# Two heads side by side in the state space mixer; split queries and keys in the neighbourhood attention

## The chip, the cores and the metric

The program runs on one core of one Trainium2 chip. A core has a matrix engine (TensorE, PE in the profile; its weight loads are listed apart as PEld), a vector engine (DVE), a scalar engine (ACT), a GpSimd engine (POOL), and DMA queues that are fed by SP, ACT and POOL. Each engine works through its own list of instructions in a fixed order and waits at semaphores for the others. The metric is the time of one execution on the device in microseconds; the kernel before has a median of 2454.5 us over three runs.

## The reference, cut to what matters

The program is a backbone of two layers over 512 latent and 256 context tokens of width 1024. Layer 0 runs a gated linear recurrence (HGRN2) and a two-dimensional neighbourhood attention beside each other, then a mixture of 16 experts. Layer 1 runs a state space mixer (SSD), then 16 experts again. The change touches the attention and the state space mixer.

In the attention every query sees a window of 8 rows by 32 columns (with a bias and a mask) and all 256 context tokens; a head has 64 channels:

```python
s_win = jnp.einsum('bhjqd,bhkjcd->bhjqkc', qr, k_band).astype(F32)
s_win = jnp.where(col_mask, s_win + bias, NEG_INF)
s_ctx = jnp.einsum('bhjqd,bhmd->bhjqm', qr, kc).astype(F32)
logits = jnp.concatenate([s_win.reshape(b, h, NA_NCB, NA_QCB, n_win), s_ctx], axis=-1)
p = jax.nn.softmax(logits, axis=-1).astype(v.dtype)
```

In the mixer each chunk's output is a masked product inside the chunk plus what the state carried in from earlier chunks gives, for 32 heads of 64 channels in 8 groups of 4, in both directions of time:

```python
seg = acum[:, :, :, None] - acum[:, :, None, :]
decay = jnp.exp(jnp.where(causal, seg, -jnp.inf))
cb = jnp.einsum('nblgk,nbsgk->nblsg', cc, bc)
y_diag = jnp.einsum('nblsgh,nbsghp->nblghp', cb[..., None] * decay * dtc[:, :, None], xc)
...
    y = y_d + jnp.einsum('blgk,bghpk->blghp', c_i, hs) * jnp.exp(a_i)[..., None]
```

The reference uses chunks of 64; the kernel uses chunks of 128, which gives the same sum.

## The kernel before, in words

All matrix products go through the helper `mm` (L76). Its operands are either float32, which the trace shows as two matrix instructions for each call, or float32r, which is one. Where a projection needs full precision in float32r, both operands are split into a high part and a remainder and three products are added (`gemm_fm`); the high part is a copy on ACT that rounds, the remainder a subtraction on DVE. A written-down order of the program isn't what runs: a scheduler with a timeline of its own reorders the instructions of each engine at build time. So the work of neighbouring pieces of the program is interleaved: the projections of the next pair of heads, or of the next group, stand between the pieces of the present one.

**Neighbourhood attention** (`for pr in range(4)`, pairs of heads). `gemm_fm` makes the pair's keys (128 channels, both heads) in two PSUM banks, one for latent and one for context tokens. They are copied to `kT` (L910, L911). The queries are made the same way and written into the tiles `qz` (L917, L919): one for each head, in which the other head's 64 partitions are zero, so that a product over 128 partitions with `kT` yields the scores of one head alone. For each of four column blocks `j` and both heads `e`, two `mm` with 256 columns each fill a bank with window and context scores (`at<-kT,qz`); then come bias, maximum, exponential, normalisation, four transposes, and the product with the values (`o<-ptT,...`), which writes head 0 to partitions 0 to 63 and head 1 to 64 to 127 of one bank, heads alternating. The context tokens' own attention is 4 more score products for each head.

**State space mixer** (`for g in range(8)`). A group's projections and convolutions come first; then GpSimd makes the weighted inputs `xw` and `xdt`, PE, GpSimd and DVE chain the states `st` over four chunks, and the output is made for each half `m` of the group (two heads), in one PSUM bank `py` (named `o` in the profile). For every head `hh` of the half and direction `d`: the cumulated decay of the head is loaded to all partitions as `R` (L1543, a DMA in ACT's queue), DVE subtracts (L1546, four instructions), ACT exponentiates `mt` (L1548) and `R` (L1550), DVE multiplies `mt` with the masked products `cb` (L1549), GpSimd multiplies `R` with `cT` (L1551), and eight `mm` with 64 stationary and 128 moving columns follow, by turns from `mt` and from `R`. All eight write the same 64 partitions. `R` and `mt` have four buffers of 512 elements.

Of the kernel before, what the change touches and what calls it, by code (L numbers as in the profile page):

```python
# [22 lines left out]
LAT = 512  # L23
# [27 lines left out]
def kernel(ctx: ExitStack, tc: tile.TileContext, A: dict, out: bass.AP):  # L51
# [23 lines left out]
    def mm(o, l, r, start, stop, **k):  # L75
        return T.matmul(o, l, r, start=start, stop=stop, skip_group_check=True, **k)  # L76
# [724 lines left out]
    with ExitStack() as mb, ExitStack() as mx:  # L801
# [46 lines left out]
        with tc.tile_pool(name="na", bufs=1, side="right") as na:  # L848
# [25 lines left out]
            qz = [[na.tile([128, TOK], F32, name=f"qz{b}{e}") for e in range(2)] for b in range(2)]  # L874
            for b in range(2):
                for e in range(2):
                    G.memset(qz[b][e], 0.0)
# [15 lines left out]
            for pr in range(4):  # L893
# [20 lines left out]
                q2 = qz[pr % 2]  # L914
                for e in range(2):
                    h = slice(e * 64, (e + 1) * 64)
                    S.mul(q2[e][h, :LAT].rearrange("p (j r q) -> p r j q", j=4, r=8)[:, ::-1],  # L917
                          pl[h, :].rearrange("p (r j q) -> p r j q", j=4, r=8), 0.125)
                    V.tensor_scalar(q2[e][h, LAT:], pc[h, :], 0.125, None, op0=ALU.mult)  # L919
                ws.ahead()  # L920

                ktl = kT[:, :LAT].rearrange("p (r c) -> p r c", c=64)
# [3 lines left out]
                for j in range(4):  # L926
# [3 lines left out]
                    for e in range(2):  # L930
                        pS = at_bank()
                        lq = q2[e][:, j * 128:(j + 1) * 128]
                        mm(pS[:, :256].rearrange("p (r c) -> p r c", c=32), lq,
                           ktl[:, :, band0[j]:band0[j] + 32], True, True)
                        mm(pS[:, 256:], lq, kT[:, LAT:], True, True)
# [22 lines left out]
                for e in range(2):  # L958
                    pS = at_bank()
                    for qt in range(2):  # L960
                        mm(pS[:, qt * 256:(qt + 1) * 256], q2[e][:, LAT + qt * 128:LAT + (qt + 1) * 128],
                           kT[:, LAT:], True, True)
# [361 lines left out]
    with ExitStack() as mb:  # L1324
# [21 lines left out]
        with ExitStack() as sx:  # L1346
# [98 lines left out]
            for g in range(8):  # L1445
# [44 lines left out]
                for d in range(2):  # L1490
                    hs = slice(d * 32 + g * 4, d * 32 + g * 4 + 4)
                    xw = sp.tile([128, NT, 256], F32, name="xw")
                    xd_ = sp.tile([128, NTL, 256], F32, tag=f"xdt{d}", name="xdt")
                    for i in range(NT):
                        if i == (3 if d == 0 else 0):
                            continue
                        G.tensor_tensor(xw[:, i, :].rearrange("p (h c) -> p h c", h=4),  # L1497
# [9 lines left out]
                    mm(p, bk[:, 4, :], xw[:, 4, :], True, False)  # L1507
                    mm(p, bk[:, 5, :], xw[:, 5, :], False, True)
# [269 lines left out]
```

## Time and profile before

| | |
|---|---|
| median of three runs | 2454.5 us (2453.52 to 2455.11) |
| profiled execution | 2452.72 us |
| its span, first to last instruction | 2451.0 us |
| mean granted clock of TensorE | 0.979 |
| PE busy | 2337.8 us, 95% of the span |
| DVE, ACT, POOL busy | 1253.8, 833.1, 552.3 us |
| neighbourhood attention | about 75 to 290 us of the span |
| state space mixer, its eight groups | about 1245 to 1860 us |

A row of the windows view gives a stretch of the span, its length, and the busy time of each engine in it with the count of instructions, then granted clock, share of DMA time and GB/s. A row of the waits view reads: who waited, for whom, total time, times, longest. A row of the timeline reads: start, length, engine, line, operation, out<-in, stationary partitions times columns, output shape, count; rows of equal instructions that overlap are merged. A row of the groups view has the count behind x, then the busy time, the mean length of one in ns, and the idle time before it. Matrix instructions are pipelined, and so their lengths overlap: what an instruction costs PE is the distance from its start to the next start, not its length.

### The profile page before, as it was taken

The numbers are of one execution on the slowest core, as the hardware profiler recorded it, in microseconds if no ns is written. First come the engines' busy times: TensorE is split into PE (matmuls) and PEld (weight loads), VectorE is DVE, ScalarE is ACT, GpSimd is POOL, SyncE is SP. The second block draws the span as 40 slices with busy tenths as digits, with TensorE's granted clock in tenths as the row PEclk, the third lists the DMA queues.
The fourth block names the chain that finished last, engine by engine and source line by source line (L and its number), as shares of the span: only waits on it lengthen the run. The fifth ranks groups of instructions, "written<-read, shape, count | busy, mean of one in ns | idle before, by whom it ended". The sixth has DMA issues, their size and how long they took to land.

```text
span 2451.0 us, 38906 instructions
## 1 busy us (share of the span) xinstructions
PE 2337.8 (95%) x16036; PEld 1519.9 (62%) x16036; DVE 1253.8 (51%) x2259; ACT 833.1 (34%) x1429; POOL 552.3 (23%) x475
## 2 busy tenths in 40 slices
PE   7999999889999999999898999999999999999997
PEld 6888788776344444434477778888878744443432
DVE  5455466636233344324787678767785612222224
ACT  4234535522333334323553334443443221111111
POOL 2000034431112222212224444444541100000001
PEclk9999999999999999999999999999999999999999
DMA  8553211248899999999523332333245989999994
GB/s 265 174 159 125 82 53 42 80 154 311 295 362 389 353 370 394 384 355 374 161 74 91 112 112 91 108 109 119 81 157 203 369 326 392 405 417 419 418 419 196
DMA packets 256929, 582.26 MB, mean 238 GB/s; under 512 B 14768, under 2 KB 129584, under 8 KB 256752
## 3 DMA queue, kind: packets, MB, share of 16 engines
q1 hardware_dynamic: 240384, 546.35, 59.3%
q0 software_dynamic: 4128, 14.68, 2.6%
q10 hardware_dynamic: 12240, 18.75, 2.5%
q8 instruction: 126, 2.06, 0.3%
q14 instruction: 51, 0.42, 0.0%
HBM read 557.32 MB, written 22.41 MB: 237 GB/s over the span
## 4 chain that ended last, share of the span: by engine, by line
PE 82%; DVE 10%; DMA 2%; ACT 2%; issue 1%; POOL 1%; SPq 0%; ACTq 0%; DVEq 0%; POOLq 0%
PE mm L76 48%; PE at L76 18%; PE o L76 7%; PE tp L76 6%; PE tp L87 3%; DVE acc L1437 1%; DVE mt L1549 1%; DVE mt L1546 1%; PE warm L76 1%; DMA w_ada<-in_ada_w_dram 0%; DMA w_moe<-in_w_dram 0%; DVE acc L409 0%; DVE w_s L726 0%; DVE cum L1051 0%; POOL xw L1497 0%
## 5 line engine op out<-in xcount | busy, mean ns | idle before, releaser
L76 PE MATMUL mm<-w_moe,xs 128*32 128x512 f32 (+1 forms) x4064 | 578.7, 594 | 0.3 <-ACT xs L435 0.3
L76 PE MATMUL mm<-xh,w_s 128*128 128x512 f32 (+2 forms) x1824 | 486.0, 362 | 9.2 <-ACT w_s L675 4.7
L76 PEld LDWEIGHTS mm<-w_moe,xs 128*32 128x32 f32 (+1 forms) x4064 | 172.5, 116 | 359.9 <-issue 347.5
L76 PEld LDWEIGHTS mm<-xh,w_s 128*128 128x128 f32 (+1 forms) x1824 | 308.3, 190 | 63.5 <-issue 6.6
L76 PE MATMUL mm<-xl,w_s 128*128 128x512 f32 (+1 forms) x912 | 294.8, 360 | 0.2 <-POOL xl L747 0.2
L76 PEld LDWEIGHTS mm<-xl,w_s 128*128 128x128 f32 x912 | 159.1, 190 | 24.2 <-issue 3.1
L76 PE MATMUL at<-w_s,hT_h 128*96 128x512 f32 x480 | 163.7, 410 | 2.4 <-DVE w_s L499 0.9
L1437 DVE SCALAR_TENSOR_TENSOR acc<-u,cwh,acc 128x770 f32<-128x770 f32 (+1 forms) x128 | 137.5, 1077 | 38.8 <-ACT acc L1434 37.6
L499 DVE TENSOR_TENSOR w_s<-w_moe,w_s 128x1024 fp32r<-128x1024 f32 x90 | 122.5, 1387 | 65.8 <-ACT w_s L498 65.7
L499 POOL TENSOR_TENSOR w_s<-w_moe,w_s 128x1024 fp32r<-128x1024 f32 x30 | 73.5, 2452 | 337.6 <-ACT w_s L498 287.9
L498 ACT CAST w_s<-w_moe 128x1024 fp32r<-128x1024 f32 x120 | 123.9, 1049 | 49.4 <-PE at L76 23.8
L1551 POOL TENSOR_TENSOR R<-R,cT 128x512 f32<-128x512 f32 x64 | 101.1, 1599 | 126.3 <-ACT R L1550 122.3
L76 PE MATMUL at<-w_moe,o 128*64 128x512 f32 x512 | 119.7, 598 | 1.6 <-ACT o L604 1.6
L461 DVE TENSOR_TENSOR ha<-mm,ha 128x512 f32<-128x512 f32 x16 | 11.1, 691 | 214.3 <-PE mm L76 213.6
L1709 POOL TENSOR_TENSOR acc<-acc,spare 128x384 f32<-128x384 f32 x4 | 4.6, 1149 | 502.0 <-ACT spare L1707 502.0
L76 PEld LDWEIGHTS at<-w_s,hT_h 128*96 128x96 f32 x480 | 76.7, 164 | 57.2 <-issue 19.4
L726 DVE TENSOR_TENSOR w_s<-w_raw,w_s 128x1024 fp32r<-128x1024 f32 x56 | 73.7, 1320 | 73.8 <-ACT w_s L725 73.6
L460 ACT ACTIVATE ha<-mm 128x512 f32<-128x512 f32 x16 | 9.6, 597 | 256.8 <-PE mm L76 256.8
L76 PE MATMUL at<-w_s,hT_l 128*96 128x512 f32 x240 | 95.5, 399 | 0.0
L76 PE MATMUL o<-R,st 128*64 128x128 f32 x512 | 94.8, 276 | 0.3 <-DVE st L1518 0.2
L76 PE MATMUL o<-mt,xdt 128*64 128x128 f32 x512 | 94.1, 277 | 0.0
L76 PE MATMUL mm<-w_s,xh 128*128 128x256 f32 x480 | 89.5, 291 | 2.5 <-ACT qs L1029 2.5
(454 smaller groups left out, 3928.1 us busy)
## 6 DMA issues: line engine op xcount, KB each, us to landing
w_moe<-in_w_dram SPq DMA_DIRECT2D x378, 1024.0 KB
w_ada<-in_ada_w_dram SPq DMA_DIRECT2D x41, 1024.0 KB
w_raw<-in_ssd_w_in_dram SPq DMA_DIRECT2D x16, 1024.0 KB
R<-acd ACTq DMA_DIRECT2D x64, 256.0 KB
w_raw<-in_ab_w_in_dram SPq DMA_DIRECT2D x12, 1024.0 KB
w_raw<-in_ssd_w_in_dram SPq DMA_DIRECT2D x16, 512.0 KB
w_raw<-in_ssd_w_out_dram SPq DMA_DIRECT2D x8, 1024.0 KB
spare<-in_ada_w_dram SPq DMA_DIRECT2D x7, 1024.0 KB
```

Source lines behind the costliest of these rows:

```text
L76: return T.matmul(o, l, r, start=start, stop=stop, skip_group_check=True, **k)
L87: return T.transpose(o, i, ident[b:b + k, b:b + k])
L460: S.activation(ha, B[0], AF.Silu)
L461: V.tensor_tensor(ha, B[1], ha, ALU.mult)
L498: S.copy(wh, w2[:, kk, :])
L499: (G if k % 4 == 3 else V).tensor_tensor(wl, w2[:, kk, :], wh.bitcast(F32), ALU.subtract)
L726: V.tensor_tensor(wl, r, wh.bitcast(F32), ALU.subtract)
L1437: V.scalar_tensor_tensor(acc[:, :n], u[:, i:i + n], cwh[:, i * 32 + cblk:i * 32 + cblk + 1], acc[:, :n], op0=ALU.mult, op1=ALU.add)
L1546: V.tensor_scalar(mt[:, c, :], R[:, c, :], acT[:, c, col:col + 1], 0.0, op0=ALU.subtract, op1=ALU.min)
L1549: V.tensor_tensor(mt, mt, cb[d], ALU.mult)
L1551: G.tensor_tensor(R, R, cT.rearrange("p (a b) -> p a b", a=4), ALU.mult)
L1709: G.tensor_tensor(x[:, FC:], x[:, FC:], fg[:, FC:], ALU.mult)
```

## The change

In the **neighbourhood attention** the zero-padded queries are gone. For each head `e` a tile `q_s[e]` holds the high part of the head's queries in the head's own 64 partitions and the remainder in the other 64, both in float32r. A tile `kk[e]` holds the high part of its keys twice, in both halves of the partitions (index 0), and the remainder twice (index 1). A product of `q_s` with index 0 and one with index 1, added in PSUM, thus give all four terms of the split product, each with one float32r instruction. For this ACT makes eight rounding copies of the keys for each pair of heads and DVE eight subtractions, all from PSUM; the queries go to a tile `qt`, and from there to `q_s` by two copies on ACT and two subtractions on DVE. `kk` and `q_s` partly live in buffers of the recurrence that follows.

In the **mixer** two heads of one direction are loaded, exponentiated and multiplied together (`R` and `mt` with 1024 elements and two buffers instead of 512 and four), and the products are written in pairs: the same chunk of head 0 (partitions 0 to 63 of the bank) and of head 1 (64 to 127) follow each other; all from `mt` first, then all from `R` in the order in which the states become ready. `xw` loses a slot that was never used.

```diff
-                kT = na.tile([128, TOK], F32, name="kT", bufs=2)
+                half = [slice(0, 64), slice(64, 128)]
+                kk = [gi.tile([128, 2, TOK], F32R, tag="v", bufs=2, name="kk") if pr % 2 == 0 else
+                      na.tile([128, 2, TOK], F32R, name=f"kk{e}") for e in range(2)]
                 pl, pc = gemm_fm(w, 128)
-                S.copy(kT[:, :LAT], pl)
-                V.tensor_copy(kT[:, LAT:], pc)
+                for p, c in ((pl, slice(0, LAT)), (pc, slice(LAT, TOK))):
+                    for e in range(2):
+                        h = half[e]
+                        for o in (h, half[1 - e]):
+                            S.copy(kk[e][o, 0, c], p[h, :])
+                        for o in (h, half[1 - e]):
+                            V.tensor_tensor(kk[e][o, 1, c], p[h, :], kk[e][h, 0, c].bitcast(F32), ALU.subtract)
...
+                q2 = [gi.tile([128, TOK], F32R, tag="z", bufs=6, name="q_s") for _ in range(2)]
+                qt_ = na.tile([128, TOK], F32, name="qt")
+                S.mul(qt_[:, :LAT].rearrange("p (j r q) -> p r j q", j=4, r=8)[:, ::-1],
+                      pl.rearrange("p (r j q) -> p r j q", j=4, r=8), 0.125)
+                V.tensor_scalar(qt_[:, LAT:], pc, 0.125, None, op0=ALU.mult)
                 for e in range(2):
...
+                    h, o = half[e], half[1 - e]
+                    S.copy(q2[e][h], qt_[h])
+                    V.tensor_tensor(q2[e][o], qt_[h], q2[e][h].bitcast(F32), ALU.subtract)
...
-                        mm(pS[:, 256:], lq, kT[:, LAT:], True, True)
+                        for f in range(2):
+                            ktl = kk[e][:, f, :LAT].rearrange("p (r c) -> p r c", c=64)
+                            mm(pS[:, :256].rearrange("p (r c) -> p r c", c=32), lq,
+                               ktl[:, :, band0[j]:band0[j] + 32], f == 0, f == 1)
+                        for f in range(2):
+                            mm(pS[:, 256:], lq, kk[e][:, f, LAT:], f == 0, f == 1)
...
-                            R = sp.tile([128, 4, 128], F32, name="R", bufs=4)
+                        R = sp.tile([128, 2, 4, 128], F32, name="R", bufs=2)
+                        S.dma_start(out=R.rearrange("p h a b -> p (h a b)"),
+                                    in_=acd[col:col + 2, :].rearrange("h t -> (h t)").partition_broadcast(128))
+                        mt = sp.tile([128, 2, 4, 128], F32, name="mt", bufs=2)
...
+                        S.activation(mt, mt, AF.Exp)
+                        V.tensor_tensor(mt, mt, cb[d].unsqueeze(1).to_broadcast([128, 2, 4, 128]), ALU.mult)
+                        S.activation(R, R, AF.Exp)
+                        G.tensor_tensor(R, R, cT.rearrange("p (a b) -> p a b", a=4).unsqueeze(1).to_broadcast([128, 2, 4, 128]),
+                                        ALU.mult)
+                        def heads(c, w, r, last):
+                            for hh in range(2):
+                                mm(py[hh * 64:(hh + 1) * 64, c, :], w[:, hm][:, hh * 64:(hh + 1) * 64], r[:, hh, c, :], False, last)
+                        for c in range(4):
+                            heads(c, xdt[d][:, c], mt, False)
+                        for n in range(4):
+                            heads(n if d == 0 else 3 - n, st[d][:, n], R, True)
```

Since a scheduler sets the order, three places show what it made of this. A row is one instruction or several equal ones that follow each other (x and their count); a number behind a name tells buffers of one name apart.

PE in the mixer, second half (`m` = 1) of the second group, before. `o_11925` is the half's bank, `mt_11929` and `R_11927` belong to head 0 and direction 0, `mt_11948` and `R_11946` to head 0 and direction 1, `mt_11967` and `R_11965` to head 1 and direction 0:

```order
L76 MATMUL o_11925<-vecT_71 128x512
L76 MATMUL o_11925<-mt_11929,xdt_11725 64x128
L76 MATMUL o_11925<-R_11927,st_11735 64x128
...
L76 MATMUL o_11925<-mt_11948,xdt_11753 64x128
L76 MATMUL o_11925<-R_11946,st_11763 64x128
...
L76 MATMUL o_11925<-mt_11967,xdt_11725 64x128
L76 MATMUL o_11925<-R_11965,st_11735 64x128
```

The same half, now (`mt_12039`, `R_12037`: both heads, direction 0; `mt_12070`, `R_12068`: both heads, direction 1):

```order
L76 MATMUL o_12035<-vecT_71 128x512
L76 MATMUL o_12035<-mt_12039,xdt_11849 64x128 x8
L76 MATMUL o_12035<-R_12037,st_11859 64x128 x8
L76 MATMUL at_12104<-ones_10825,ysq_12031 128x1
L76 MATMUL mm_12255<-xl1_10582,w_s_12190 128x512
...
L76 MATMUL o_12035<-mt_12070,xdt_11877 64x128 x8
L76 MATMUL o_12035<-R_12068,st_11887 64x128 x8
```

Eight products of one direction now stand together, head 0 and head 1 by turns, and both directions have a run of sixteen each.

PE in the mixer, first half (`m` = 0) of the second group, now; `at` is the step of the state chain, `mm` the projection of the third group:

```order
L76 MATMUL o_11966<-mt_11970,xdt_11849 64x128 x8
L76 MATMUL o_11966<-R_11968,st_11859 64x128 x2
L76 MATMUL tp_12176<-sel_101,ada_row_12174 128x4
L76 MATMUL at_11872<-xw_11848,bk_11573 128x256
L76 MATMUL o_11966<-R_11968,st_11859 64x128 x4
L76 MATMUL mm_12193<-xh1_10581,w_s_12187 128x512
...
L76 MATMUL o_11966<-R_11968,st_11859 64x128 x2
L76 MATMUL o_11966<-mt_12001,xdt_11877 64x128 x3
```

The products from `R` wait for one state each, and so they stand in twos and fours between products of other shapes. Over the whole mixer the 512 products stood in 60 unbroken runs before and stand in 82 now; 506 of them are in neighbouring pairs of the two heads.

PE in the neighbourhood attention, first pair of heads, now (`mm_1363` and `mm_1364` are the key projection of the second pair):

```order
L76 MATMUL at_1027<-kk_864,q_s_985 128x256 x4
L76 MATMUL mm_1364<-xh_113,w_s_994 128x256
L76 MATMUL mm_1363<-xl_114,w_s_994 128x512
L76 MATMUL at_1047<-kk_865,q_s_986 128x256 x4
L76 MATMUL mm_1364<-xl_114,w_s_994 128x256
```

Four float32r products stand where two float32 products stood. Ahead of the first of these rows stand the 24 products with 512 columns of the first query projection, and then, behind the query projection, 19 products with 512 columns and 18 with 256 of the second key projection.

More of the change, by code (lines that the diff above doesn't have):

```diff
@@ L873 @@
             nvr = nvd.rearrange("(r c) d -> r c d", c=64)
[L874 to L877, printed above, removed]
             def softmax_tail(pS, nm, n):
@@ L960 @@
                     for qt in range(2):
-                        mm(pS[:, qt * 256:(qt + 1) * 256], q2[e][:, LAT + qt * 128:LAT + (qt + 1) * 128],
-                           kT[:, LAT:], True, True)
+                        for f in range(2):
+                            mm(pS[:, qt * 256:(qt + 1) * 256], q2[e][:, LAT + qt * 128:LAT + (qt + 1) * 128],
+                               kk[e][:, f, LAT:], f == 0, f == 1)
                     nm = na.tile([128, 2], F32, name="nm", bufs=3)
@@ L1506 @@
                     p = at_bank([128, 256])
[L1507 to L1508 removed]
+                    mm(p, bk[:, 4, :], xw[:, at_[4], :], True, False)
+                    mm(p, bk[:, 5, :], xw[:, at_[5], :], False, True)
                     S.copy(s[:, 0, :], p)
@@ L1537 @@
                     clear(py)
-                    for hh in range(2):
-                        for d in range(2):
-                            h = m * 2 + hh
-                            col = d * 32 + g * 4 + h
-                            R = sp.tile([128, 4, 128], F32, name="R", bufs=4)
-                            S.dma_start(out=R.rearrange("p a b -> p (a b)"), in_=acd[col:col + 1, :].to_broadcast([128, LAT]))
-                            mt = sp.tile([128, 4, 128], F32, name="mt", bufs=4)
+                    hm = slice(m * 128, (m + 1) * 128)
@@ L1545 @@
+                    for d in range(2):
+                        col = d * 32 + g * 4 + m * 2
+                        R = sp.tile([128, 2, 4, 128], F32, name="R", bufs=2)
[3 more added lines that the diff above has]
+                        for hh in range(2):
                             for c in range(4):
-                                V.tensor_scalar(mt[:, c, :], R[:, c, :], acT[:, c, col:col + 1], 0.0,
+                                V.tensor_scalar(mt[:, hh, c, :], R[:, hh, c, :], acT[:, c, col + hh:col + hh + 1], 0.0,
@@ new lines @@
+                        V.tensor_tensor(mt, mt, cb[d].unsqueeze(1).to_broadcast([128, 2, 4, 128]), ALU.mult)
[3 more added lines that the diff above has]
+                        def heads(c, w, r, last):
+                            for hh in range(2):
+                                mm(py[hh * 64:(hh + 1) * 64, c, :], w[:, hm][:, hh * 64:(hh + 1) * 64], r[:, hh, c, :], False, last)
```

29 lines of the change are left out of this document (5 added, 24 removed).

## The prediction

> **What bounds the kernel now.** I read the page first: which engine is busy, and where.
>
> ```profile
> span 2451.0 us, 38906 instructions
> PE 2337.8 (95%) x16036; PEld 1519.9 (62%) x16036; DVE 1253.8 (51%) x2259; ACT 833.1 (34%) x1429; POOL 552.3 (23%) x475
> ```
>
> PE is busy for 95% of the span. As an average that says little, so next the windows of the stages that the change touches, and of what follows them:
>
> ```profile
> core 0: us, PE busy (x) PEld busy (x) DVE busy (x) ACT busy (x) POOL busy (x), PEclk, DMA share, GB/s
> 75.00:290.00 215.00, 215.00 (x1763) 175.86 (x1763) 107.20 (x242) 84.08 (x177) 0.00 (x0) 1.00 0.43 135
> 1300.00:1860.00 560.00, 540.52 (x3459) 450.85 (x3460) 424.57 (x690) 228.26 (x396) 247.23 (x247) 0.98 0.34 111
> 1860.00:2451.00 591.00, 561.81 (x2903) 272.32 (x2901) 180.70 (x371) 98.73 (x182) 17.87 (x20) 0.97 0.90 363
> ```
>
> In the attention (75 to 290) PE has no idle time at all; in the mixer (1300 to 1860) it idles for 19.5 of 560 us. DVE is next, with 50% and 76%. The last stage carries its own load of weights (DMA share 0.90); it begins when the mixer ends, and the change only moves it. Third, the waits, to see whether PE or its suppliers come last:
>
> ```profile
> DVE at L936 <- PE at L76: 19.7, 18, 3.3
> ...
> PE at L1576 <- DVE rs_y L142: 7.7, 3, 3.8
> PE mm L76 <- DVE w_s L676: 4.4, 1, 4.4
> PE at L76 <- POOL xw L1497: 3.4, 3, 1.4
> PE at L76 <- DVE st L1518: 2.9, 4, 1.3
> ```
>
> In the attention DVE waits for PE's scores, and no wait of PE is listed. In the mixer PE's few waits are for the group norm (`rs_y`), one split of weights and the state chain (`xw`, `st`). So a microsecond less of PE work is worth nearly a microsecond in the attention, and less than that in the mixer, where DVE isn't far behind.
>
> **The change in the mixer.** It moves 512 products and removes none. What does one cost PE, alone and in a run?
>
> ```profile
> 1332.34 0.38 PE L76 MATMUL o<-mt,xdt 128*64 128x128 f32 x2
> 1332.55 0.38 PE L76 MATMUL o<-R,st 128*64 128x128 f32 x2
> 1332.77 0.38 PE L76 MATMUL o<-mt,xdt 128*64 128x128 f32 x2
> ...
> 1492.94 0.43 PE L76 MATMUL o<-mt,xdt 128*64 128x128 f32 x2
> ...
> 1497.94 0.39 PE L76 MATMUL mm<-xh,w_s 128*128 128x256 f32 x1
> ...
> 1851.41 0.84 PE L76 MATMUL mm<-w_s,y_s 128*128 128x512 f32 x3
> 1852.18 0.43 PE L76 MATMUL o<-mt,xdt 128*64 128x128 f32 x2
> 1852.54 0.73 PE L76 MATMUL mm<-w_s,y_s 128*128 128x512 f32 x2
> ```
>
> Inside a run one product (two instructions) follows another after 0.22 us. Alone it costs more: the last of the three products with 512 columns starts at 1851.41 + 0.84 - 0.39 = 1851.86 and would take 0.23 (the spacing in a projection, below), the next starts at 1852.54, which leaves 0.45. Entering and leaving a run thus costs 0.45 - 0.22 = 0.23. The run of 24 from 1492.94 to 1497.94 took 5.00 where 24 x 0.22 + 0.14 (the leaving) would be 5.42: at the one place where the head changes, 0.4 is saved. Before, the order has 60 runs with 16 such places: 512 x 0.22 + 60 x 0.23 - 16 x 0.4 = 113 + 14 - 6 = 121 us.
>
> What products of two heads by turns cost is in the trace already, at the same shape: the attention's value products alternate between partitions 0 to 63 and 64 to 127 of one bank.
>
> ```profile
> 142.00 0.54 PE L76 MATMUL o<-ptT,vb 128*64 128x128 f32 x5
> 142.28 0.27 PE L76 MATMUL o<-ptT,nvc 128*64 128x128 f32 x1
> 142.38 0.27 PE L76 MATMUL o<-ptT,vb 128*64 128x128 f32 x1
> 142.38 0.70 PE L76 MATMUL o<-ptT,nvc 128*64 128x128 f32 x7
> 143.02 0.55 PE L87 MATMUL tp<-ident,pe 128*128 128x128 f32 x3
> 142.28 0.57 PEld L76 LDWEIGHTS o<-ptT,nvc 128*64 128x64 f32 x7
> ```
>
> Fourteen instructions, seven products, in 1.02 us: that is the four products of the longer side alone, 4 x 0.22 + 0.14 = 1.02; one after another the seven would take 1.68. The other side costs nothing. Now 506 of the 512 products stand in such pairs, in 82 runs: 259 x 0.22 + 82 x 0.23 = 57 + 19 = 76 us. PE saves 121 - 76 = **45 us**; the 22 added runs are 5 us of the 76.
>
> [...]
>
> The work ahead of the products gets fewer, longer instructions. The nearest rows for 1024 elements are those of the weight splits:
>
> ```profile
> L1551 POOL TENSOR_TENSOR R<-R,cT 128x512 f32<-128x512 f32 x64 | 101.1, 1599 | 126.3 <-ACT R L1550 122.3 <-PE mm L76 3.0 <-DVE rs_t L137 0.6
> L726 DVE TENSOR_TENSOR w_s<-w_raw,w_s 128x1024 fp32r<-128x1024 f32 x56 | 73.7, 1320 | 73.8 <-ACT w_s L725 73.6
> L499 POOL TENSOR_TENSOR w_s<-w_moe,w_s 128x1024 fp32r<-128x1024 f32 x30 | 73.5, 2452 | 337.6 <-ACT w_s L498 287.9 <-DVE hT_l L480 29.3 <-PE at L76 20.5
> L1549 DVE TENSOR_TENSOR mt<-mt,cb 128x512 f32<-128x512 f32 x64 | 66.1, 1066 | 0.4 <-ACT mt L1548 0.4
> L725 ACT CAST w_s<-w_raw 128x1024 fp32r<-128x1024 f32 x56 | 58.3, 1048 | 74.9 <-PE mm L76 55.7 <-PE at L76 17.6 <-PE o L76 1.5
> L1550 ACT ACTIVATE R<-R 128x512 f32<-128x512 f32 x64 | 39.6, 618 | 0.0
> L1546 DVE TENSOR_SCALAR mt<-R,acT 128x128 f32<-128x128 f32 x256 | 71.0, 340 | 23.8 <-DMA R<-acd 22.8 <-PE at L76 0.9
> ```
>
> GpSimd's product with `cT` goes from 64 x 1.60 to 32 x 2.45, 101 to 78 us; DVE's with `cb` from 66 to 32 x 1.32 = 42; the two exponentials from 128 x 0.62 to 64 x 1.05, 79 to 67. The 256 subtractions stay, the loads become 32. All of that lies beside PE: worth nothing by itself, but it keeps DVE from becoming the bound. Of 424.6 us DVE keeps some 401, against a mixer of 560 - 45 = 515 us: 78%. The cover gets thinner all the same: PE comes to the same producers 45 us earlier in sum, and waited 19.5 us for them already. How much that grows no row tells; bounds are nothing and all 45. I take half as much again as the present waits, rounded up to 12, since DVE, ACT and GpSimd each get less work: **33 us** of gain.
>
> **The change in the attention.** 80 float32 score products (160 instructions of 256 columns) become 160 float32r ones.
>
> ```profile
> 93.00 1.02 PE L76 MATMUL at<-kT,qz 128*128 128x256 f32 x4
> ...
> 94.34 0.40 PE L76 MATMUL mm<-xl,w_s 128*128 128x512 f32 x1
> 94.58 0.63 PE L76 MATMUL mm<-xh,w_s 128*128 128x512 f32 x2
> ...
> 1331.02 0.40 PE L76 MATMUL mm<-xh,w_s 128*128 128x256 f32 x2
> 1331.26 0.28 PE L76 MATMUL mm<-xl,w_s 128*128 128x256 f32 x1
> ...
> L628 DVE TENSOR_TENSOR y_s<-m,y_s 64x512 fp32r<-64x512 f32 x32 | 21.2, 684 | 3.6 <-ACT y_s L627 3.1
> ```
>
> The four instructions at 93.00 last 1.02, one lasts 0.38, so the step is 0.213 and an old product 0.43. Two float32r instructions with 256 columns start 0.40 - 0.28 = 0.12 apart, so the two that replace it cost 0.24. 80 x 0.19 = 15 us less. Outside the mixer's 82 runs the new order changes the array's shape 18 more times, at about half of 0.23 each: 2 us. That leaves **13 us**.
>
> The added copies are the price. For each pair of heads ACT gets eight casts of at most 0.6 us (618 ns for 512 elements), one scaling of 0.6 and two casts of 768 elements (between 0.6 and 1.05), DVE eight subtractions of at most 0.68, a short scaling below that and two subtractions of 768 elements (between 0.68 and 1.32): about 7 and 8 us, and times four, with nothing taken off for today's copies, 28 and 32 us. DVE then has at most 107 + 32 = 139 of about 202 us, ACT 84 + 28 = 112: neither is the bound. On the path lie the keys: from the end of their projection some 6 us (eight subtractions and the first cast) instead of 0.6. In that time PE runs the latent query products, 24 x 0.23 = 5.6 us, and the context ones, which need a bank that the first half of the subtractions frees. Then the queries: scaling, cast, two subtractions and a weight split that stands before them on DVE, 0.6 + 0.8 + 2.0 + 1.3 = 4.7 us, under 19 x 0.23 + 18 x 0.12 = 6.5 us of the next pair's projection. Both are covered, by a microsecond or two; without this cover four pairs times 10 us would stand open. The float32r tiles in the recurrence's buffers cost nothing: their first two pairs are read long before the recurrence fills those buffers.
>
> **Sum.** 2452.7 (the profiled execution; 1.7 of it outside the span) - 33 - 13 = 2406.7. The median of the runs is 1.8 above the profiled execution: **2408 us**.
>
> **The rivals.** *The mixer's waits eat most of it.* The state chain and R's chain (after the load eight subtractions, two exponentials and GpSimd's product: 8 x 0.34 + 2 x 1.05 + 2.45 = 7.3 us) keep their length while the work that covers them gets shorter; the 22.8 us that DVE already waits for `R` speak for it, DVE's 78% against. With a third of the 45 us left: 2454.5 - 15 - 13 = 2427.
>
> *All of it arrives.* Nothing waits longer, since three engines were relieved: 2454.5 - 45 - 15 = 2394, and a few us below if the 7.7 us at `rs_y` shrink as well.
>
> [...]
>
> *Slower: the load of R at the head of ACT's queue.* With two buffers each load waits until PE has read the pair before last, and behind it in ACT's queue stand the copies out of the projections' banks, whose banks PE needs for its cover. PE then waits for a load that waits for PE. It turns slower once each of the 32 loads costs more than 46 / 32 = 1.4 us; at 2 us the time is 2408 + 64 = 2472. Against it: before, four single buffers held the same two pairs, and ACT waited for `R` only 11.8 us in all.
>
> ```profile
> ACT w_s L675 <- DMA R<-acd: 6.9, 1, 6.9
> ACT xg L1441 <- DMA R<-acd: 4.9, 1, 4.9
> ```
>
> **How the numbers follow.** Forecast (2395 to 2420) 0.60; waits eat most 0.20; all arrives 0.10; no side by side 0.04; slower 0.06. A measurement of this kernel can tell 0.2%, 5 us, from no change. All cases but the last are faster by more; of the slower one I give a third to a time within 5 us. Faster 0.94, same 0.02, slower 0.04. The range takes in the second and third case, 2386 to 2436.
>
> **What would show it.** Right: in the mixer, rows `o<-mt` and `o<-R` that start in twos 0.22 us apart for two products, runs of 16 in about 1.9 us; a mixer of about 525 us between the same events; score rows 0.12 us apart, and still no PE wait in the attention, which ends 13 us earlier. Wrong: waits of PE for `R`, `mt`, `st` or `u` that add up to more than 32 us in the mixer; PE waiting for `kk` or `q_s` in the attention; ACT rows that end on a wait for PE behind a load of `R`.

## The result and the profile after

The changed kernel takes 2401.4 us (median of four executions, 2395.8 to 2403.0) beside 2454.0 us for the kernel before on the same chip (2452.1 to 2455.1): a ratio of 0.9782, 95% interval 0.9765 to 0.98. Timed once more, with the last experiments, it took 2404.0 us (2400.2 to 2406.0) beside 2452.0: 0.9796, interval 0.9783 to 0.981. The forecast was 2408 us, range 2386 to 2436: the sign, the two sources of the gain and the range were right, and the gain was 48 to 53 us instead of 46.

The page of the changed kernel, first its span, then busy time by engine:

```profile
span 2394.1 us, 38699 instructions
PE 2278.7 (95%) x16036; PEld 1453.1 (61%) x16036; DVE 1264.8 (53%) x2259; ACT 851.3 (36%) x1403; POOL 546.4 (23%) x439
```

PE is busy 59.1 us less than before (2337.8), and idle 2394.1 - 2278.7 = 115.4 us instead of 113.2. So nearly all of the saved work arrived. Where? The same program events cut both executions into stretches: first score product, last score product, first expert product, first subtraction for `mt`, last product from `R`, end. The windows view of the kernel before (columns: stretch, its length, then busy time and instructions of PE, PEld, DVE, ACT and POOL, the granted clock of PE, DMA share, GB/s):

```profile
93.00:271.50 178.50, 178.50 (x1509) 145.35 (x1508) 96.03 (x223) 69.69 (x156) 0.00 (x0) 1.00 0.45 143
271.60:622.80 351.20, 324.69 (x2763) 267.06 (x2761) 200.51 (x422) 137.32 (x211) 105.76 (x94) 0.97 0.35 119
622.90:1277.10 654.20, 633.68 (x4506) 300.84 (x4507) 291.14 (x438) 249.95 (x399) 152.93 (x80) 0.98 0.88 326
1277.20:1858.20 581.00, 558.12 (x3602) 463.73 (x3600) 443.28 (x725) 240.62 (x418) 262.50 (x263) 0.98 0.35 112
1858.30:2450.90 592.60, 563.51 (x2909) 273.71 (x2909) 182.37 (x373) 99.39 (x183) 17.87 (x20) 0.97 0.90 362
```

The same five stretches of the changed kernel:

```profile
99.40:275.00 175.60, 175.58 (x1588) 145.94 (x1587) 111.24 (x247) 93.16 (x191) 0.00 (x0) 1.00 0.45 142
275.10:608.60 333.50, 307.32 (x2650) 251.75 (x2648) 200.30 (x420) 133.74 (x205) 107.20 (x94) 0.96 0.35 122
608.70:1260.40 651.70, 632.19 (x4506) 299.94 (x4507) 293.21 (x438) 250.21 (x399) 152.35 (x80) 0.98 0.88 327
1260.50:1800.30 539.80, 519.19 (x3622) 411.87 (x3621) 433.61 (x695) 235.89 (x356) 259.43 (x231) 0.99 0.37 121
1800.40:2394.00 593.60, 558.80 (x2890) 269.08 (x2888) 179.00 (x372) 97.84 (x181) 16.90 (x20) 0.98 0.90 361
```

The experts begin 622.9 - 608.7 = 14.2 us earlier; that is the attention's part. The scores themselves start 6.4 us later than before. That is work and not waiting: up to there PE has 34 more instructions (x752 before, x786 now) and is busy 6.3 us longer (78.9, 85.2), with as much idle time as before (14.0, 14.1). The gain appears behind the scores, where that work is now missing (x2763 to x2650). The mixer is 41.2 us shorter, 38.9 of it PE's busy time, and its idle time went from 22.9 to 20.6 us. Some of the 38.9 may be clock: in the mixer the granted clock was one half for 26 us before and for 14 now (18 in the second execution), counted in windows of 2 us; half of the difference, 4 to 6 us, is an estimate of what that is worth. The two stretches that the change doesn't touch are 2.5 us shorter and 1.0 us longer.

The timeline of the changed kernel shows the new steps (start, length, engine, line, operation, count):

```profile
99.36 0.64 PE L76 MATMUL at<-kk,q_s 128*128 128x256 f32 x4
99.84 0.28 PE L76 MATMUL mm<-xh,w_s 128*128 128x256 f32 x1
...
1563.47 0.44 PE L76 MATMUL o<-R,st 128*64 128x128 f32 x4
1563.74 1.04 PE L76 MATMUL o<-mt,xdt 128*64 128x128 f32 x16
1564.71 0.62 PE L76 MATMUL mm<-xh,w_s 128*128 128x512 f32 x2
```

Four score instructions take 0.64 with the last at about 0.28: 0.12 apart. Ten products of two heads by turns (twenty instructions) take 1564.71 - 1563.47 = 1.24 us, which is 5 x 0.22 and 0.14 to leave the run.

PE's two largest waits in the changed kernel's mixer (total, times, longest):

```profile
PE at L1592 <- DVE rs_y L142: 6.1, 3, 4.4
PE at L76 <- POOL xw L1507: 3.3, 3, 2.0
```

and right behind the mixer, two that the kernel before doesn't have there:

```profile
PE mm L87 <- DVE x_res L1668: 2.0, 1, 2.0
...
PE mm L76 <- ACT y_s L1608: 1.7, 1, 1.7
```

No row of PE in the mixer names `R` or `mt`, the smaller ones included. The two waits behind the mixer are new, 3.7 us, and give back a part of the mixer's gain. The work ahead of the products, in the mixer of the changed kernel:

```profile
L1563 POOL TENSOR_TENSOR R<-R,cT 128x1024 f32<-128x1024 f32 x32 | 90.7, 2845 | 97.1 <-ACT R L1562 75.3 <-DVE w_s L676 10.1 <-DVE xg L1452 10.0
L1558 DVE TENSOR_SCALAR mt<-R,acT 128x128 f32<-128x128 f32 x256 | 62.7, 314 | 17.0 <-DMA R<-acd 17.0
...
L1561 DVE TENSOR_TENSOR mt<-mt,cb 128x1024 f32<-128x1024 f32 x32 | 54.7, 1727 | 2.8 <-ACT mt L1560 2.8
```

The merged instructions are longer than forecast (2.85 us instead of 2.45 on POOL, 1.73 instead of 1.32 on DVE), and DVE is busy for 434 of the mixer's 540 us, 80%.

### The profile page after: what moved, and what is told of

Its sections match the earlier page's. It is cut to its first block, busy times and chain, and to the rows that moved or that the text cites. A ratio compares the mean times of both kernels' runs of the same rounds, so it can differ in the third digit from the quotient of the medians.

```text
span 2394.1 us, 38699 instructions
## 1 busy us (share of the span) xinstructions
PE 2278.7 (95%) x16036; PEld 1453.1 (61%) x16036; DVE 1264.8 (53%) x2259; ACT 851.3 (36%) x1403; POOL 546.4 (23%) x439
## 5 line engine op out<-in xcount | busy, mean ns | idle before, releaser
L461 DVE TENSOR_TENSOR ha<-mm,ha 128x512 f32<-128x512 f32 x16 | 11.1, 691 | 211.7 <-PE mm L76 211.0
L1563 POOL TENSOR_TENSOR R<-R,cT 128x1024 f32<-128x1024 f32 x32 | 90.7, 2845 | 97.1 <-ACT R L1562 75.3
L597 DVE TENSOR_TENSOR ha<-mm,ha 128x512 f32<-128x512 f32 x16 | 11.1, 692 | 138.1 <-PE mm L76 138.1
L1507 POOL TENSOR_TENSOR xw<-xk,weT 128x256 f32<-128x256 f32 x80 | 63.3, 816 | 87.2 <-ACT xk L1484 83.1
```

The source lines that it names most:

```text
L461: V.tensor_tensor(ha, B[1], ha, ALU.mult)
L597: V.tensor_tensor(ha, B[1], ha, ALU.mult)
L1507: G.tensor_tensor(xw[:, n, :].rearrange("p (h c) -> p h c", h=4), xk[:, i, :].rearrange("p (h c) -> p h c", h=4), weT[:, i, hs].unsqueeze( ...
L1563: G.tensor_tensor(R, R, cT.rearrange("p (a b) -> p a b", a=4).unsqueeze(1).to_broadcast([128, 2, 4, 128]), ALU.mult)
```

## The experiments

The theory: PE sets the end in both places, so its product time arrives, and the producers have just enough room. The rivals: the pairs aren't what helps, but the longer instructions ahead of them; the room is wide; or the producers are already the bound.

### One part alone

The two parts, each with the other as it was before.

> The mixer's part alone; the attention as before. Theory (matrix work saved is time saved, and the two parts add): the mixer's 41 us of the profiled 57 remain, 2411 to 2418 us, that is 14 to 16 us above the changed kernel's 2401. Rival (most of it is the attention's, because what follows starts earlier): above 2425.

> The attention's part alone; the mixer as before. Theory: 13 to 16 us faster than before, 2438 to 2441. Rival (the added copies eat it, the earlier start of the recurrence came from elsewhere): 2450 to 2460.

Timed beside them the kernel before took 2455.2 us. The mixer alone: 2423.6 us, ratio 0.9868 (0.985 to 0.9885), 31.6 us less. The attention alone: 2444.6 us, ratio 0.9954 (0.9937 to 0.9971), 10.6 us less. The theory's range for the mixer was missed by 6 us, that for the attention by 3.6. The windows view of the attention alone, the stretch that begins with the first expert product:

```profile
609.50:1264.30 654.80, 635.00 (x4506) 303.78 (x4507) 292.78 (x438) 249.75 (x399) 152.16 (x80) 0.98 0.88 325
```

The experts begin at 609.5, 13.4 us earlier than before; the rest is lost behind that, in stretches that the change doesn't touch. The two parts add up to 42 us, ten less than both at once in the first timing, which the last experiments take up.

### The order of the products, without the pairs

`R` and `mt` stay merged for two heads, but the products are written head after head:

```diff
-                        for c in range(4):
-                            heads(c, xdt[d][:, c], mt, False)
-                        for n in range(4):
-                            heads(n if d == 0 else 3 - n, st[d][:, n], R, True)
+                        for hh in range(2):
+                            for c in range(4):
+                                heads(c, xdt[d][:, c], mt, False, hh)
+                        for hh in range(2):
+                            for n in range(4):
+                                heads(n if d == 0 else 3 - n, st[d][:, n], R, True, hh)
```

> Both parts, with R and mt for two heads at once, but the products of one half written one head after the other. If the gain of the mixer comes from two heads running side by side: the products cost 512 x 0.22 + 84 x 0.23 less at most 95 x 0.4 for the places where the scheduler put the two heads next to each other, 94 to 132 us instead of 76, so 2420 to 2450. If it comes from the fewer, longer instructions on ACT, DVE and GpSimd: within 5 us of 2401.

2413.9 us (2413.3 to 2419.1), ratio 0.983 (0.9813 to 0.9847): 12 us slower than the changed kernel, below the pairs theory's 2420 and far outside the other's 2406. Taking the pairs out of the text doesn't take them all out of the order: the scheduler put 95 neighbouring products of opposite heads together by itself, as the expectation had allowed for. The mixer of this kernel:

```profile
1264.40:1823.70 559.30, 537.87 (x3601) 433.32 (x3598) 427.87 (x694) 236.45 (x355) 253.33 (x231) 0.98 0.35 116
```

Adding up, for each product, the time from its start to the next instruction's start, without PE's waits and with 0.09 for each run entered (an estimate: 0.23 for entering and leaving a run in the kernel before, less 0.14 for leaving), gives 102.8 us here, 78.8 in the changed kernel and 121.5 before. The mixer is 559.4, 539.9 and 581.1 us long. So 24.0 us of PE's product time are worth 19.5 us of the mixer, 17.4 beside the changed kernel's second execution (541.9 us). The side-by-side products are what helps. The medians differ by 12 us alone; why a third of the mixer's difference doesn't reach them is open, and what the clock does to single executions (below) is as large.

### Pairs, without the merged preparation

The other half alone: products in pairs, `R` and `mt` as tiles of one head with four buffers, as before.

```diff
-                        R = sp.tile([128, 2, 4, 128], F32, name="R", bufs=2)
-                        mt = sp.tile([128, 2, 4, 128], F32, name="mt", bufs=2)
+                        for hh in range(2):
+                            R = sp.tile([128, 4, 128], F32, name="R", bufs=4)
+                            mt = sp.tile([128, 4, 128], F32, name="mt", bufs=4)
...
-                                mm(py[hh * 64:(hh + 1) * 64, c, :], w[:, hm][:, hh * 64:(hh + 1) * 64], r[:, hh, c, :], False, last)
+                                mm(py[hh * 64:(hh + 1) * 64, c, :], w[:, hm][:, hh * 64:(hh + 1) * 64], r[hh][:, c, :], False, last)
```

> Both parts, with the products in pairs, but R and mt for one head at a time in four buffers as before. If pairs are the gain: 93 runs instead of 82, 3 us more, and about 20 us more on GpSimd, DVE and ACT each that stay beside PE: 2401 to 2410. If the longer instructions were needed so that PE's suppliers keep up: waits of PE in the mixer grow by 10 us and more, 2412 to 2430.

2396.1 us (2393.5 to 2399.3), ratio 0.9763 (0.9744 to 0.9781), below both expectations. The mixer:

```profile
1262.30:1799.90 537.60, 518.09 (x3603) 408.62 (x3601) 444.33 (x724) 240.44 (x417) 257.24 (x263) 0.99 0.37 120
```

It is 2 us shorter than the changed kernel's, though DVE has 11 us more to do (444 of 538 us, 83%), PE waits 2.5 us for `mt`, and the products stand in 93 runs instead of 82 (84.4 us of product time). The merged tiles and their longer instructions bring nothing.

### How thin the cover is in the attention

The casts and subtractions that build the keys, each done twice:

```diff
-                        for o in (h, half[1 - e]):
+                        for o in (h, half[1 - e], h, half[1 - e]):
                             S.copy(kk[e][o, 0, c], p[h, :])
-                        for o in (h, half[1 - e]):
+                        for o in (h, half[1 - e], h, half[1 - e]):
                             V.tensor_tensor(kk[e][o, 1, c], p[h, :], kk[e][h, 0, c].bitcast(F32), ALU.subtract)
```

> The changed kernel with each of the eight casts and eight subtractions that build the keys' tiles of a pair of heads done twice: by the changed kernel's rows 0.48 us x 8 = 3.8 us more of ScalarE and 0.56 us x 8 = 4.5 us more of VectorE for each of the four pairs, 15 and 18 us in all, and the keys of a pair ready some 4 to 5 us later. Theory 'the added copies lie beside TensorE's work with a us or two to spare', as forecast: TensorE then waits 2 to 3 us a pair for the keys, 8 to 12 us in all, 2409 to 2414 us. Rival 'the cover is wide, since the order holds other work between a projection and its scores': within 3 us of 2401, and no row of TensorE that waits for the keys. Rival 'the copies are already on the path': the whole 15 to 18 us, 2416 to 2420 us.

2427.2 us (2424.5 to 2433.1), ratio 0.9896 (0.9875 to 0.9917) beside 2453.5: slower than all three expectations, and so at the end of the rival that puts the copies on the path. The scores' stretch, and PE's largest wait in the attention:

```profile
104.10:295.50 191.40, 184.67 (x1620) 153.62 (x1618) 125.37 (x270) 107.80 (x216) 0.00 (x0) 0.98 0.40 128
```

```profile
PE mm L76 <- DVE qt L923: 5.7, 3, 3.8
```

PE waits not for the keys but one step further on: the scaling of the context queries (`qt`) stands in DVE's queue behind the added subtractions, and until it has read the projection's bank, PE can't go on with the next projection. The experts begin at 630.6, 22 us later than in the changed kernel; PE's idle time up to there grew by 16.5 us, about the length of the added copies (ACT's busy time grew by 15.4, DVE's by 16.7); 6.3 of it lies behind the scores. The changed kernel itself has no wait of PE there. So the cover is nearly used up: the first round of copies fits, and the second shows as idle time of PE, nearly whole.

### How thin it is in the mixer

One more instruction on DVE for each pair of heads and direction:

```diff
                         V.tensor_tensor(mt, mt, cb[d].unsqueeze(1).to_broadcast([128, 2, 4, 128]), ALU.mult)
+                        V.tensor_scalar(mt, mt, 1.0, None, op0=ALU.mult)
```

> The changed kernel with one VectorE instruction more for each pair of heads and direction in the mixer: the decay tile of 128x1024 multiplied by 1.0, in place, between the multiplication by cb and the products. An instruction of this kind on 128x128 takes 0.31 us, the multiplication of the same tile by cb 1.73 us, so between 1.0 and 1.7 us each, 32 to 55 us of VectorE in all: its share of the mixer's 540 us goes from 80% (433.6 us) to 86 to 91%. Theory 'in the mixer TensorE alone sets the end, and what prepares its tiles has room': the stage grows by at most 5 us, 2401 to 2407 us. Rival, the step of the forecast that let TensorE's waits grow by half as VectorE's and POOL's shares come nearer to TensorE's: waits grow by another 12 us or more, 2413 us and up.

2427.9 us (2424.5 to 2432.9), ratio 0.9892 (0.9875 to 0.9908): 26 us slower than the changed kernel, the rival's side. The added group (lines view), the largest wait of PE in the mixer, and the mixer's window:

```profile
L1562 DVE TENSOR_SCALAR mt<-mt 128x1024 f32<-128x1024 f32 x32 | 46.7, 1465 | 0.1
```

```profile
PE o L76 <- DVE mt L1562: 11.7, 5, 2.8
```

```profile
1266.90:1833.60 566.70, 532.35 (x3630) 422.09 (x3628) 473.54 (x727) 234.76 (x356) 268.50 (x231) 0.96 0.36 115
```

40 us more on DVE (473.5 instead of 433.6) make the mixer 27 us longer. Of that 13.7 us are idle time of PE (34.3 instead of 20.6), and now PE waits for `mt`. The other 13.2 are PE's busy time, for nearly the same instructions (x3630, x3622): PE itself is slower, with a granted clock of 0.96 instead of 0.99. The windows of the changed kernel show how, around its longest wait for `rs_y`:

```profile
1342.00:1344.00 2.00, 0.62 (x10) 0.36 (x10) 1.90 (x4) 1.24 (x3) 1.15 (x1) 1.00 0.00 0
1344.00:1346.00 2.00, 0.00 (x0) 0.00 (x0) 1.97 (x2) 0.00 (x0) 2.00 (x2) 0.97 0.00 0
1346.00:1348.00 2.00, 0.42 (x2) 0.43 (x3) 2.00 (x2) 0.00 (x0) 1.50 (x1) 0.50 0.00 0
1348.00:1350.00 2.00, 2.00 (x12) 2.00 (x10) 1.39 (x3) 0.00 (x0) 0.00 (x0) 0.50 0.00 0
1350.00:1352.00 2.00, 2.00 (x25) 1.32 (x25) 1.70 (x4) 0.11 (x1) 0.00 (x0) 0.50 0.35 131
1352.00:1354.00 2.00, 2.00 (x30) 1.78 (x33) 2.00 (x3) 0.53 (x2) 0.17 (x1) 0.82 0.36 36
```

PE waits 4.4 us, the granted clock (the third number from the end) falls to 0.50 before the wait is over, and stays there for about 5 us after PE has begun again: 6.8 us in all. Counted in such windows, the changed kernel's 15 stretches below full clock ahead of its last microseconds are 3.4, 6.8 or 10.2 us long; in windows of 0.25 us the clock reads 1.00 or 0.50, but for the windows at their edges. PE's steps lengthen with it: 22 instructions `tp<-w_ada,sT` from 1350.33 on, at 0.50, take 1.43 us (0.065 each), 30 from 1353.39 on, at 1.00, take 1.01 (0.034 each). So this wait costs its 4.4 us and then, as an estimate from those steps, up to half of the 5 us that follow. In the mixer of the changed kernel such stretches add up to 14 us, here to 45.

The run doesn't tell why `mt` comes late. The added instruction raises DVE's load, and it also stands between load and product of every tile and makes that way 1.5 us longer. With single-head tiles DVE was busy for 83% of the mixer, here for 84%, and there the mixer lost nothing; so the share of DVE alone doesn't set the edge. An instruction of the same length beside the chain wasn't tried.

### One buffer of `R`

The recorded slower rival, made as strong as it can be:

```diff
-                        R = sp.tile([128, 2, 4, 128], F32, name="R", bufs=2)
+                        R = sp.tile([128, 2, 4, 128], F32, name="R", bufs=1)
```

> The changed kernel with one buffer instead of two for R, the tile of two heads' decay rows: the next load of R waits in ScalarE's queue until the products with the last one are done, and everything behind it on ScalarE waits too. This is the recorded slower rival ('R's load at the head of ScalarE's queue') with its wait made as long as it can be. If that mechanism has a price near the one of the forecast (2 us for each of 32 tiles), the stage grows by 60 us or more: 2460 us and up. If the tiles are prepared so far ahead that a load's wait is covered by half, 2415 to 2435 us. Theory 'TensorE sets the end and there is slack on every engine that feeds it': the 13 fewer runs that the order shows for it (69 instead of 82) save 3 us and the waits cost under 10: 2398 to 2410 us.

2471.8 us (2467.7 to 2478.3), ratio 1.0084 (1.0062 to 1.0107): 70 us slower than the changed kernel and slower than before. From its page and its waits in the mixer:

```profile
L1558 DVE TENSOR_SCALAR mt<-R,acT 128x128 f32<-128x128 f32 x256 | 57.4, 295 | 70.6 <-DMA R<-acd 70.6
```

```profile
PE o L76 <- DVE mt L1561: 25.1, 8, 7.9
PE mm L76 <- ACT w_s L675: 11.1, 3, 4.7
```

DVE waits 70.6 us for `R` (17.0 with two buffers), PE 25.1 for `mt`, and 11.1 for a weight split on ACT, where the loads are issued. So a load that waits for PE does come back to PE, at 2.2 us of time for each of the 32 loads; with two buffers no wait of PE for `mt` or `R` is listed. Whether it comes through ACT's queue, as the rival had it, or only because each tile is prepared later, isn't separated: one buffer with the loads in another queue wasn't run.

### Without the second score product

```diff
-                        for f in range(2):
+                        for f in range(1):
...
-                               ktl[:, :, band0[j]:band0[j] + 32], f == 0, f == 1)
+                               ktl[:, :, band0[j]:band0[j] + 32], True, True)
...
-                        for f in range(2):
-                            mm(pS[:, 256:], lq, kk[e][:, f, LAT:], f == 0, f == 1)
+                        mm(pS[:, 256:], lq, kk[e][:, 0, LAT:], True, True)
```

> The changed kernel's scores without the product with the keys' remainder: of each two float32r products in the neighbourhood attention only the first is left, 80 products instead of 160; all tiles are still built. This leaves out a part of the scores and tells what the second product costs. Theory 'TensorE sets this stage, each such product is 0.12 us': 80 x 0.12 = 9.6 us less, 2390 to 2393 us. Rival 'the stage is now held by the softmax between two scores, so TensorE's saving no longer arrives': 2399 to 2403 us, with waits of TensorE in the attention.

The edit reached 64 products, not 80 (the context queries' scores stand elsewhere), so 7.7 us were to be had. 2401.9 us (2399.9 to 2405.1), ratio 0.9795 (0.9779 to 0.9811): nothing arrives. First score to first expert product, in this kernel and in the changed one:

```profile
99.80:606.40 506.60, 474.80 (x4175) 390.43 (x4173) 311.22 (x668) 228.05 (x396) 106.74 (x94) 0.97 0.39 130
```

```profile
99.40:608.60 509.20, 483.00 (x4236) 397.79 (x4234) 311.55 (x667) 226.90 (x396) 107.20 (x94) 0.97 0.38 129
```

PE has 8.2 us less to do, as it should, but the stretch is only 2.6 us shorter, and its idle time went from 26.2 to 31.8. PE's waits where the recurrence opens, without the second product:

```profile
PE tp L87 <- DVE kin L1086: 4.3, 1, 4.3
PE mm L76 <- ACT z L1038: 4.1, 1, 4.1
```

The time is in the rival's range, but not by its mechanism: no wait of PE stands in the scores. What grew stands at the start of the recurrence behind the attention, which needs ACT and DVE first: in the changed kernel the wait for `z` is already there with 3.7 us, and that for `kin` is new. A further saving in the scores thus hardly arrives.

### The changed kernel and the mixer alone, again

> The changed kernel as it is, to see how far its time and the places of its stretches at half the granted clock belong to the kernel. Its first trace has 89 us at a granted clock of 0.50, in 16 places, each a multiple of 3.4 us, behind waits of TensorE; the trace with the mixer changed alone has 112 us in 23 places. If the places belong to the program: 86 to 92 us again and a median of 2399 to 2403 us. If each execution draws them anew: anything between 80 and 112 us, and single times that spread over 8 us or more.

> The kernel with the mixer changed alone, a second time, beside the changed kernel itself. Its time was 2423.6 us, 31.6 below before, and that of the attention alone 10.6 below; together 42, where both at once gave 53. If the missing 10 us are the stretches at half clock, and these belong to each program: 2421 to 2426 us again with 108 to 115 us at half clock. If they are drawn anew by each execution: a median nearer to 2414 us, which is 2401 and the 13 us that the attention gives before the mixer begins.

The changed kernel: 2404.0 us (2400.2 to 2406.0). The mixer alone: 2418.7 us (2415.8 to 2420.4), ratio 0.9859 (0.9844 to 0.9874), 33.3 below before, and 4.9 below its own first time. Neither expectation of the first holds whole: the median is just above 2403, and the stretches at half clock add up to 104 us, not 86 to 92, but the single times spread over 5.7 us, not 8. The second's 2418.7 lies between its two expectations. Span and mean granted clock of the changed kernel's two profiled executions; those of the mixer alone have 2422.9 us at 0.977 and 2416.5 at 0.980:

```profile
core 0: 2394.1 us, clock 0.981
```

```profile
core 0: 2403.6 us, clock 0.978
```

One program gives two executions 9.5 and 6.4 us apart, each time with the lower clock in the longer one. Counted in windows of 2 us the changed kernel has 89 and 104 us at half clock, the mixer alone 112 and 95. By the estimate from PE's steps at 0.50 and at 1.00 the difference is worth up to half of it, 8 us each. So the stretches aren't fixed by the program, though most come at the same waits (12 of the 15 that the changed kernel's first execution has ahead of its last microseconds come back in the second). That each execution draws them wholly anew isn't shown either: the four times of the mixer alone lay at 2421.9 to 2424.6 first and at 2415.8 to 2420.4 now, without overlap, but on another chip, and the kernel before moved as well (2455.2 and 2452.0).

With the second timings the ten missing microseconds shrink to 48 - 33 - 11 = 4, less than one execution differs from the next. And the mixer alone shows where a part of its own gain goes. In the second execution its mixer takes 541.4 us, 39.6 less than before, but the last stretch, 592.6 us before, is 8.1 longer:

```profile
1815.70:2416.40 600.70, 565.46 (x2890) 274.00 (x2888) 178.06 (x372) 97.98 (x181) 16.88 (x20) 0.97 0.89 357
```

PE's idle time in it is 35.2 us instead of 29.1; the waits for `x_res` and `y_s` are 3.8 of that.

### Single-head tiles, again

> Products in pairs, with R and mt as tiles of one head in four buffers, a second time, beside the changed kernel itself. Its first median was 2396.1 us, from another call than the changed kernel's 2401.4. If it is truly the faster of the two: 3 to 7 us below the changed kernel in this call. If not: within 2 us of it.

2397.2 us (2393.8 to 2401.9), ratio 0.9776 (0.9761 to 0.979): 6.7 us below the changed kernel timed beside it, after 5.3 in the first timings. Both times it is the faster of the two, by 0.2 to 0.3%, though its interval overlaps with that of the changed kernel. From its page:

```profile
span 2395.5 us, 38958 instructions
PE 2282.9 (95%) x16036; PEld 1457.5 (61%) x16036; DVE 1272.9 (53%) x2291; ACT 857.5 (36%) x1467; POOL 547.5 (23%) x471
```

and the changed kernel's, in its second profiled execution:

```profile
span 2403.6 us, 38699 instructions
PE 2285.7 (95%) x16036; PEld 1459.8 (61%) x16036; DVE 1264.1 (53%) x2259; ACT 850.3 (35%) x1403; POOL 545.4 (23%) x439
```

PE is idle 112.6 us instead of 117.9; the waits for `y_s` and `x_res` behind the mixer are not there. They aren't there in the next kernel either, which keeps the merged tiles and comes out in another order; so the size of the tiles alone doesn't make them, and what does wasn't tried.

### `R` loaded from another queue

```diff
-                        S.dma_start(out=R.rearrange("p h a b -> p (h a b)"),
+                        SY.dma_start(out=R.rearrange("p h a b -> p (h a b)"),
```

> The changed kernel with R loaded by SP's queue instead of ScalarE's; nothing else is changed. VectorE waits 17.0 us for R's transfer in the mixer of the changed kernel, in 17 places, and with one buffer of R the kernel took 2472 us. Theory 'with two buffers the load's place in ScalarE's queue costs nothing that reaches TensorE': within 4 us of the changed kernel in this call. Rival 'ScalarE is held by the load': VectorE's wait for R halves and the kernel is 5 to 12 us faster. A rival on the other side: SP's queue holds the weights' loads behind it, and the kernel is 5 us slower or more, with TensorE waiting for w_s.

2401.6 us (2393.8 to 2403.5), ratio 0.9785 (0.9768 to 0.9802), 2.4 us below the changed kernel timed beside it: within the theory's 4 us, and the two ranges overlap. DVE's wait for `R` in this kernel, total and times:

```profile
  DMA R<-acd: 20.3, 14
```

It didn't halve (17.0 in 17 places with ACT's queue), so with two buffers ACT's queue isn't what the loads wait for. The rival on the other side, loads of weights held up in SP's queue, fell too: the kernel isn't slower, and PE waits 0.6 us for `w_s` in the mixer.

## Why the prediction was right

**The products in the mixer: right.** Forecast 121 us before (its terms, added unrounded, give 120), 76 after, 45 saved; measured 121.5, 78.8 and 42.7, at the forecast step of 0.22 us for two products. Products of two heads by turns do run side by side at this shape: ten in 1.24 us, where ten of one head, at the 0.22 us each of the kernel before, would take 10 x 0.22 + 0.14 = 2.34 by estimate. Taking the written pairs away, with all else kept, cost 12 us.

**The growth of PE's waits by 12 us: mis-sized, and this is the step that failed.** The forecast let the waits grow by half as much again as the mixer's 19.5 us. PE's idle time grew by 2.2 us in the whole execution, and by 4.7 in the second profiled one (117.9 instead of 113.2). In the mixer it fell, from 22.9 to 20.6 (21.2 in the second); what grew stands behind it (`y_s`, `x_res`). The 7 to 10 us between 12 and these are more than the 1.6 to 6.1 us by which the gain over the kernel before, timed beside it, exceeds the forecast's 46.5 (48.1 and 52.6); the products gave 2 us less than forecast, and the rest is within what the clock does to single executions. The reason given for the growth, "the cover gets thinner", was sound all the same: 32 more instructions on DVE, 40 us in all, produced just such waits for `mt`. The forecast put the edge too near. Whether DVE's load or the longer way of each tile makes that edge isn't separated.

**The preparation: right that it is worth nothing by itself, wrong in its sizes.** POOL's product with `cT` takes 91 us in the mixer, not 78, and DVE's with `cb` 55, not 42, so of the 24 us of relief on DVE 10 are left (443 to 434 us). Single-head tiles do as well or better.

**The attention: right.** Forecast 15 less 2 for changes of shape, 13 us; PE's busy time up to the first expert product fell by 14.0 us (78.9 + 178.5 + 324.7 to 85.2 + 175.6 + 307.3), the experts begin 14.2 us earlier, and the attention alone gave 10.6 us in the median and 13.4 in that stretch. "Covered, by a microsecond or two" was right too: there is no PE wait in the scores, and doubling the keys' copies put nearly all of the added length on the path. The 2 us for changes of shape weren't measured apart. What the forecast did not see is that this place has little more to give: of 8 us less in the scores 2.6 were left at the first expert product and nothing in the median.

**The rivals.** "Waits eat most" fell: 2 to 5 us of waits, not 30. "All of it arrives" (2394) lies 7 and 10 us below the two medians, where the forecast lies 7 and 4 above them: the times don't choose between these two, and PE's idle time, 2 to 5 us more instead of 12, is nearer to the rival. "No side by side" (chance 0.04), two heads' products by turns costing as much as one after another, fell. The slower one, 2472, didn't come with two buffers. With one the time is 2471.8; that the figures agree is chance, since the forecast priced another kernel.

**What the prediction left out** is the granted clock, which it took as the same before and after. Counted in the same windows the kernel before has 101 us at half clock, the changed one 89 and 104, and the spans fell by 56.9 and 47.4 us. Two profiled executions of one program thus differ by up to 10 us, and a sum made against a single one can't be tested closer than that.

## What to carry to other kernels

Where PE sets the end, products with 64 stationary columns are worth pairing by the half of the partitions that they write: here two cost the time of one, 0.22 us. Before adding copies beside such work, see how much idle time the covering engines have right there, and test the edge by doubling them, since the first round may fit and the second not at all (here it cost 16.5 us of idle time of PE). And merge the preparation only if it is on the path; longer instructions brought nothing here (2404.0 us, beside 2397.2 with the shorter ones).

## What the runs showed of the hardware that was not expected

A wait of PE can cost more than its length: with the 4.4 us for `rs_y` in the changed kernel come 6.8 us at a granted clock of 0.50, and the others of its stretches at that clock, ahead of its last microseconds, are 3.4, 6.8 or 10.2 us long. Idle time of PE (span less busy time) and time at half clock (from the mean clock: twice what is missing to 1, times the span) go together: 115 and 91 us in the changed kernel, 118 and 106 in its second execution, 134 and 136 with DVE's added instruction, 168 and 163 with one buffer of `R`. They don't go one for one: 135 and 112 with the keys built twice. The rows for DVE's added instruction and for one buffer, span with clock, and PE's busy time:

```profile
core 0: 2431.2 us, clock 0.972
```

```profile
PE 2297.4 (94%) x16036; PEld 1466.6 (60%) x16036; DVE 1303.1 (54%) x2291; ACT 849.7 (35%) x1403; POOL 555.1 (23%) x439
```

```profile
core 0: 2466.0 us, clock 0.967
```

```profile
PE 2298.2 (93%) x16036; PEld 1473.2 (60%) x16036; DVE 1254.0 (51%) x2259; ACT 851.4 (35%) x1403; POOL 539.2 (22%) x439
```

What makes a given wait start such a stretch in one execution and not in the next was not tested.
